# Seven block products in place of eight for the up products of five FFNs on one core

## The chip, the cores and the metric

One core of one Trainium2 chip runs the whole program. The metric is the device time in microseconds (us) of one execution. The engines are named as in the profile: PE multiplies matrices (PEld is its weight loads), ACT is ScalarE, DVE is VectorE, POOL is GpSimd, and SP issues the transfers.

## What is computed

Two transformer layers and one further block run on 512 tokens of width 1024 (a context of 256 tokens is used in the first layer). Six feed-forward networks (FFNs, here 0 to 5) carry most of the arithmetic:

```
D_MODEL = 1024
SEQ = 512
D_FF = 2816
def swiglu(h, wi, wo):
    a, u = jnp.split(h @ wi, 2, axis=-1)
    return (jax.nn.silu(a) * u) @ wo
```

`h @ wi` is the up product (1024 to 2 x 2816), `@ wo` the down product. Between the FFNs stand a mixer of attention and a recurrent part, a pooling mixer and a second mixer. Each layer is steered by modulation vectors, `silu(cond) @ w_mod`, 216 columns of 128 in all (the kernel calls their work ada).

## The kernel before

All activations lie transposed: 128 features on the partitions, tokens along a row. A product in float32 is made of three matmuls (`mm3`, L181 to L184): weight high part times activation high part, weight high part times activation low part, weight low part times activation high part. High parts are made by ACT (a copy into fp32r, L177 for weights, L187 for activations), low parts by DVE as the difference (L178, L188). So every weight tile takes one ACT and one DVE instruction.

An FFN (`ffn`, L331) works through 22 blocks f of 128 hidden columns in four parts of 5, 5, 6 and 6 blocks. In a part it first makes the up products of its blocks (`run`, `up`), then the down products of that part for eight slices d of the output (`downs`). For a block, `up` multiplies eight input chunks by two 128-column halves (gate and up) and three terms: 48 matmuls of 512 columns into two PSUM banks (tile `pau`). Then `gate` (L357, L358, L187, L188) applies silu, multiplies and splits the result into `g`. A block's weights arrive in two transfers of 512 KB (`load_raw`, tile `wraw`, four buffers with the tag `raw`), and `split_w` makes `whi` and `wlo` of 1024 columns from each. The ada work (`ada_step`: one 512 KB load into a buffer of the same tag, one dot product on DVE over 1024 columns, L124) is spread over the blocks, two for each. FFNs 1 to 5 have only the stream x of 512 tokens; FFN 0 also has the context.

A scheduler orders the instructions of each engine. Each engine then runs its queue strictly in that order, so an instruction that waits holds everything behind it. Transfers are issued by SP, in one queue.

## Time and profile before

| what | us |
| --- | --- |
| median of 3 runs | 3187.15 |
| lowest and highest run | 3186.84, 3192.39 |
| the profiled execution, its own time | 3192.12 |
| its span, first to last instruction | 3190.3 |
| PE busy in the span | 3074.2 |
| DVE, ACT, POOL busy | 1764.8, 1144.0, 272.8 |

How to read it: the profile lists each engine's busy time, groups of equal instructions with the mean time of one and the idle time before them, and a chain that is followed back from the last instruction. An engine's instructions in order of time show when each started and how long it took. A matmul's listed time contains its passage through the array, so PE's pace is read from the distance of starts. All rows are from the one profiled execution.

### The profile page before, as it was taken

What the parts mean: (1) busy time and instruction counts of PE and PEld (TensorE: products, weight loads), DVE (VectorE), ACT (ScalarE), POOL (GpSimd) and SP (SyncE); (2) the same over time, 40 slices, a digit from 0 to 9 for tenths busy, and PEclk for the clock granted to TensorE, in tenths of its full rate; (3) what the DMA queues carried; (4) which work ended last, traced back from release to release, by engine and by line L of the source; (5) the groups of instructions that cost most, each with busy time, mean ns of one, the idle gap of its engine ahead of it and who ended that gap; (6) DMA issues with size and microseconds to landing.
All of it is one profiled execution on the core that took longest, in us unless ns stands there. A gap on an engine that the chain in (4) does not pass through costs nothing.

```text
span 3190.3 us, 41925 instructions
## 1 busy us (share of the span) xinstructions
PE 3074.2 (96%) x16678; PEld 2585.4 (81%) x16678; DVE 1764.8 (55%) x2952; ACT 1144.0 (36%) x1904; POOL 272.8 (9%) x263
## 2 busy tenths in 40 slices
PE   6899999999899999999997999999999999999998
PEld 4788888888678888888886888888888898788887
DVE  8875535535765555655457545555533557843334
ACT  4532212433543222522234322253223556632222
POOL 4300000211100000100003000010000221110000
PEclk8999999999999999999998999999999999999999
DMA  5653525111113454445451345534433221112331
GB/s 218 240 185 105 172 90 162 56 57 54 47 41 107 157 175 162 128 156 165 145 192 47 123 155 171 174 109 147 159 99 109 78 67 54 59 58 92 107 99 62
DMA packets 118040, 381.59 MB, mean 120 GB/s; under 512 B 13490, under 2 KB 17458, under 8 KB 117844
## 3 DMA queue, kind: packets, MB, share of 16 engines
q1 hardware_dynamic: 117844, 378.91, 36.7%
q8 instruction: 131, 2.15, 0.3%
q14 instruction: 65, 0.53, 0.1%
HBM read 376.76 MB, written 2.10 MB: 119 GB/s over the span
## 4 chain that ended last, share of the span: by engine, by line
PE 86%; DVE 8%; ACT 3%; issue 2%; POOL 1%; DMA 1%; DVEq 0%; ACTq 0%; POOLq 0%; SPq 0%
PE pau L183 15%; PE pau L184 15%; PE pau L182 15%; PE py L182 8%; PE py L183 8%; PE py L184 8%; PE pj L668 1%; PE pj L669 1%; PE pj L670 1%; PE pj L183 1%; PE pj L182 1%; PE pc L182 1%; PE pc L183 1%; PE pc L184 1%; PE pj L184 1%
## 5 line engine op out<-in xcount | busy, mean ns | idle before, releaser
L182 PE MATMUL pau<-hx,whi 128*128 128x512 f32 (+1 forms) x2272 | 864.9, 382 | 22.3 <-ACT hx L187 10.7
L183 PE MATMUL pau<-hx,whi 128*128 128x512 f32 (+1 forms) x2272 | 868.3, 382 | 6.5 <-DVE hx L188 4.4
L184 PE MATMUL pau<-hx,wlo 128*128 128x512 f32 (+1 forms) x2272 | 867.1, 382 | 0.0
L177 ACT ACTIVATE whi<-wraw 128x1024 fp32r<-128x1024 f32 (+2 forms) x538 | 510.2, 954 | 930.7 <-PE py L183 446.7
L178 DVE TENSOR_TENSOR wlo<-wraw,whi 128x1024 fp32r<-128x1024 f32 (+2 forms) x538 | 591.0, 1103 | 320.4 <-ACT whi L177 311.2
L182 PEld LDWEIGHTS pau<-hx,whi 128*128 128x128 f32 x2272 | 432.7, 191 | 110.8 <-ACT hx L187 12.0
L183 PEld LDWEIGHTS pau<-hx,whi 128*128 128x128 f32 x2272 | 433.5, 191 | 96.0 <-DVE hx L188 6.7
L184 PEld LDWEIGHTS pau<-hx,wlo 128*128 128x128 f32 x2272 | 433.4, 191 | 87.7 <-DVE wlo L178 0.4
L182 PE MATMUL py<-g,whi 128*128 128x512 f32 (+1 forms) x1376 | 492.1, 358 | 9.2 <-DVE x L371 7.1
L183 PE MATMUL py<-g,whi 128*128 128x512 f32 (+1 forms) x1376 | 489.2, 356 | 1.1 <-DVE g L188 1.1
L184 PE MATMUL py<-g,wlo 128*128 128x512 f32 (+1 forms) x1376 | 488.6, 355 | 0.0
L124 DVE CUSTOM_DVE_ANT_0 junk<-adaw,cv_c,cst 128x1024 bf16<-128x1024 f32 x192 | 246.5, 1284 | 204.5 <-DMA adaw<-in_ada 203.3
L371 DVE SCALAR_TENSOR_TENSOR x<-py,gate,x 128x512 f32<-128x512 f32 (+1 forms) x216 | 149.0, 690 | 290.3 <-PE py L184 289.4
L182 PEld LDWEIGHTS py<-g,whi 128*128 128x128 f32 x1376 | 259.2, 188 | 53.1 <-ACT hc L281 5.7
L183 PEld LDWEIGHTS py<-g,whi 128*128 128x128 f32 x1376 | 259.4, 189 | 41.2 <-DVE g L188 1.4
L184 PEld LDWEIGHTS py<-g,wlo 128*128 128x128 f32 x1376 | 259.1, 188 | 40.5
L357 ACT ACTIVATE sl<-pau 128x512 f32<-128x512 f32 x132 | 78.9, 598 | 519.0 <-PE pau L184 518.8
L358 DVE TENSOR_TENSOR sl<-sl,pau 128x512 f32<-128x512 f32 x132 | 90.7, 687 | 298.5 <-PE pau L184 279.4
L216 POOL TENSOR_TENSOR acc<-acc,sq 128x512 f32<-128x512 f32 (+1 forms) x33 | 43.1, 1309 | 2309.5 <-ACT sq L214 2309.3
L187 ACT ACTIVATE g<-sl 128x512 fp32r<-128x512 f32 (+1 forms) x154 | 92.4, 601 | 112.6 <-DVE sl L358 110.6
L668 PE MATMUL pj<-whi,hx 128*128 128x256 f32 x448 | 129.3, 289 | 0.3 <-ACT vtok L675 0.3
L669 PE MATMUL pj<-whi,hx 128*128 128x256 f32 x448 | 126.5, 282 | 0.0
(417 smaller groups left out, 3630.6 us busy)
## 6 DMA issues: line engine op xcount, KB each, us to landing
wraw<-in_wi SPq DMA_DIRECT2D x274, 512.0 KB, 3.4
adaw<-in_ada SPq DMA_DIRECT2D x192, 512.0 KB, 3.8
wraw<-in_wo SPq DMA_DIRECT2D x96, 384.0 KB, 3.1
wraw<-in_wo SPq DMA_DIRECT2D x104, 320.0 KB, 3.0
wraw<-in_w_in SPq DMA_DIRECT2D x42, 512.0 KB, 3.4
adas<-in_ada SPq DMA_DIRECT2D x32, 512.0 KB, 6.2
wraw<-in_w_out SPq DMA_DIRECT2D x16, 512.0 KB, 3.4
wraw<-in_ada SPq DMA_DIRECT2D x8, 512.0 KB, 4.1
```

The costliest lines, as they stand in the source:

```text
L124: V.tensor_tensor_reduce(junk, raw, cvec(vec), 1.0, C(f"b{l}", c, 1), OP.mult, OP.add, mods[dst][:, c:c + 1])
L177: S.activation(hi, raw, AF.Copy)
L178: V.tensor_tensor(lo, raw, hi.bitcast(F32), OP.subtract)
L182: PE.matmul(o, wh, xh, start=start, stop=False)
L183: PE.matmul(o, wh, xl, start=False, stop=False)
L184: return PE.matmul(o, wl, xh, start=False, stop=stop)
L187: a = S.activation(hi, src, AF.Copy)
L357: S.activation(sl, o[0], AF.Silu)
L358: V.tensor_tensor(sl, sl, o[1], OP.mult)
L371: V.scalar_tensor_tensor(s.x[d][:, c0:c1], py[:, :c1 - c0], s.gate[:, d:d + 1], s.x[d][:, c0:c1], op0=OP.mult, op1=OP.add)
L668: PE.matmul(o, xh, hi[:, k % 4, :], start=k == 0, stop=False)
L669: PE.matmul(o, xl, hi[:, k % 4, :], start=False, stop=False)
```

## The change

In parts 1 to 3 of FFNs 1 to 5 a block's up product is treated as a 2 by 2 block matrix product: weights a11, a21 (gate and up columns of input chunks 0 to 3), a12, a22 (of chunks 4 to 7), and activations cut into chunks 0 to 3 and 4 to 7 by tokens 0 to 255 and 256 to 511. Seven products of 256 columns are made (`seven`), each of 4 chunks and 3 terms, so 84 matmuls of 256 columns stand where 48 of 512 stood. Their operands are sums:

- `combine_h`, once in an FFN, makes eight combined activation tiles (`todd`, `teven`) in part 0: for each of four k, four instructions on POOL, two on DVE, and two splits.
- `weight_sums`, once for a block, makes four sums of weight tiles (`ws`) on POOL, each 128x512.
- `form` splits the seven weight tiles of a block (three raw, four sums), 128x512 each, on ACT (L405) and DVE (L406). Form i of the next block is made behind product i of this one.
- Behind the products, ACT copies four partial results out of PSUM (L431 to L439), since one bank (`ba`) collects products 0, 2, 4 and 6 one after the other; DVE adds two and multiplies one (L437, L442, L446), POOL adds one and multiplies one (L440, L444).

One ada step goes with each of these blocks and one with each down slice of parts 0 to 2. The tile `g` has 6 buffers in place of 7. Some small pads and the buffer count of one vector change too.

```
     def gate(s, f, o):
...
+        def combine_h(k):
...
+            b1, b2, odd, even = (tmp([T], name="tc") for _ in range(4))
+            for b, c in ((b1, k), (b2, 4 + k)):
+                hh = hs["x"][c].bitcast(F32)
+                G.tensor_tensor(b, hh[:, 0], hh[:, 1], OP.add)
+            lo_, hi_ = slice(0, 256), slice(256, 512)
+            G.tensor_tensor(odd[:, lo_], b1[:, hi_], b1[:, lo_], OP.subtract)
+            V.tensor_tensor(even[:, lo_], b2[:, hi_], odd[:, lo_], OP.subtract)
+            G.tensor_tensor(odd[:, hi_], b2[:, hi_], b1[:, hi_], OP.subtract)
+            V.tensor_tensor(even[:, hi_], b2[:, lo_], even[:, lo_], OP.subtract)
+            for src, name in ((odd, "odd"), (even, "even")):
+                split(src, tt[name][k][:, 0], tt[name][k][:, 1])
+
+        def weight_sums(f):
+            w0, w1 = (load_raw(A[f"wi{n}"][f, p], [4, 2, 128]) for p in range(2))
+            a11, a21, a12, a22 = w0[:, :, 0], w0[:, :, 1], w1[:, :, 0], w1[:, :, 1]
+            s1, s2, s3, s4 = (tt["pool"].tile([128, 4, 128], F32, name="ws", tag="ws", bufs=4) for _ in range(4))
+            G.tensor_tensor(s1, a21, a22, OP.add)
+            G.tensor_tensor(s2, s1, a11, OP.subtract)
+            G.tensor_tensor(s3, a11, a21, OP.subtract)
+            G.tensor_tensor(s4, a12, s2, OP.subtract)
+            return [a11, s1, s2, a12, s3, s4, a22]
+
+        def form(src):
+            if not slot:
+                t = [wp.tile([128, 2, 4, 128], F32R, name=nm, tag=nm, bufs=4) for nm in ("whi", "wlo")]
+                slot.extend([(t[0][:, i], t[1][:, i]) for i in range(2)])
+            hi, lo = slot.pop(0)
+            S.activation(hi, src, AF.Copy)
+            V.tensor_tensor(lo, src, hi.bitcast(F32), OP.subtract)
+            return hi, lo
+
+        def seven(f, w, then):
...
+            def product(i, o, start):
+                hi, lo = w[i]
+                for k in range(4):
+                    mm3(o, hi[:, k], lo[:, k], mv[i](k, 0), mv[i](k, 1), start and k == 0, k == 3, not start)
+
+            for i, (o, start) in enumerate(((ba, True), (bc, True), (ba, False), (bd, True), (ba, False), (bc, False),
+                                            (ba, False))):
+                product(i, o, start)
+                with tc.high_priority():
+                    if i == 0:
+                        S.activation(q1[:, first], ba, AF.Copy)
+                    elif i == 1:
+                        S.activation(q1[:, second], bc, AF.Copy)
+                    elif i == 2:
+                        S.activation(q2[:, first], ba, AF.Copy)
+                    elif i == 3:
+                        V.tensor_tensor(a[:, first], bd, q1[:, first], OP.add)
+                    elif i == 4:
+                        S.activation(q2[:, second], ba, AF.Copy)
+                        G.tensor_tensor(q1[:, second], q1[:, second], q2[:, second], OP.add)
+                    elif i == 5:
+                        V.tensor_tensor(a[:, second], bc, q2[:, first], OP.add)
+                        S.activation(a, a, AF.Silu)
+                        G.tensor_tensor(a[:, second], a[:, second], q1[:, second], OP.mult)
+                    else:
+                        V.tensor_tensor(a[:, first], a[:, first], ba, OP.mult)
+                        ins = split(a, g[:, 0, :], g[:, 1, :])
+                then(i)
+            return ins
...
+                    if not cx:
+                        for k in {2: (0, 1), 3: (2,), 4: (3,)}[f]:
+                            combine_h(k)
                     ada_step(steps if X in ss and not (start and pi == 0) else 0, last_gate, pi == 0 and f == 2)
+
+            def run_seven(fs):
+                nonlocal last_gate
+                del slot[:]
+                src = weight_sums(fs[0])
+                w = [form(x) for x in src]
+                for f in fs:
+                    nxt_w = []
+                    src = weight_sums(f + 1) if f + 1 in fs else []
+                    last_gate = seven(f, w, lambda i: nxt_w.append(form(src[i])) if src else None)
+                    ada_step(1, last_gate)
+                    w = nxt_w
...
                     hi, lo = load_w(A[f"wo{n}_{pi}"][d], [nk, 128])
+                    if not cx and not last:
+                        ada_step(1)
...
-            run(todo)
+            if pi and not cx:
+                run_seven(fs)
+            else:
+                run(todo)
+            if last and not cx:
+                closed(f"tt{n}")
```

Three queues show the order around the second block of part 1 of FFN 1. In the rows `wraw` is a raw weight tile, `ws` a sum, `sq7` the partial results of a block, `pau` and `pd` its PSUM banks, `adaw` an ada column. First DVE, before, around the gate (L358, L188) of a block of that part:

```order
L178 TENSOR_TENSOR wlo_9190<-wraw_9187,whi_9189 128x1024
L358 TENSOR_TENSOR sl_9173<-sl_9173,pau_9124 128x512
L124 ISA junk_9333,mod_c1_76<-adaw_9331,cv_c_8764,cst_67 128x1024
L124 ISA mod_c1_76 128x1
L188 TENSOR_TENSOR g_9174<-sl_9173,g_9174 128x512
L178 TENSOR_TENSOR wlo_9196<-wraw_9193,whi_9195 128x1024
L124 ISA junk_9337,mod_c1_76<-adaw_9335,cv_c_8764,cst_67 128x1024
L124 ISA mod_c1_76 128x1
```

and DVE after, in the later half of the second block (the rows named 9392), up to the first two forms of the block after next:

```order
L437 TENSOR_TENSOR sq7_9392<-pd_9389,sq7_9390 128x256
L124 ISA junk_9653,mod_c1_76<-adaw_9651,cv_c_8807,cst_67 128x1024
L124 ISA mod_c1_76 128x1
L406 TENSOR_TENSOR wlo_9473<-ws_9381,whi_9472 128x512
L406 TENSOR_TENSOR wlo_9473<-ws_9382,whi_9472 128x512
L442 TENSOR_TENSOR sq7_9392<-pau_9388,sq7_9391 128x256
L446 TENSOR_TENSOR sq7_9392<-sq7_9392,pau_9387 128x256
L406 TENSOR_TENSOR wlo_9509<-wraw_9377,whi_9508 128x512
L406 TENSOR_TENSOR wlo_9509<-wraw_9516,whi_9508 128x512
L189 TENSOR_TENSOR g_9393<-sq7_9392,g_9393 128x512
L406 TENSOR_TENSOR wlo_9564<-ws_9520,whi_9563 128x512
L406 TENSOR_TENSOR wlo_9564<-ws_9521,whi_9563 128x512
```

A block had four pieces of its own and two dot products on DVE; it has eleven and one. POOL before, in FFN 1: the norm ahead of it (`mt`) is followed at once by the squares of its last down slices (`acc`), so POOL has nothing in parts 1 to 3 up to there:

```order
L275 TENSOR_TENSOR mt_8502<-x3_81,rs_y_8485 128x256
L275 TENSOR_TENSOR mt_8511<-x5_83,rs_y_8485 128x256
L275 TENSOR_TENSOR mt_8520<-x7_85,rs_y_8485 128x256
L216 TENSOR_TENSOR acc_10810<-acc_10810,sq_10847 128x512
L216 TENSOR_TENSOR acc_10810<-acc_10810,sq_10882 128x512
L216 TENSOR_TENSOR acc_10810<-acc_10810,sq_10917 128x512
```

POOL after, in the same second block (the L440 and L444 of 9392) and the start of the third:

```order
L394 TENSOR_TENSOR ws_9520<-wraw_9516,wraw_9518 128x512
L395 TENSOR_TENSOR ws_9521<-ws_9520,wraw_9516 128x512
L440 TENSOR_TENSOR sq7_9390<-sq7_9390,sq7_9391 128x256
L396 TENSOR_TENSOR ws_9522<-wraw_9516 128x512
L397 TENSOR_TENSOR ws_9523<-wraw_9518,ws_9521 128x512
L444 TENSOR_TENSOR sq7_9392<-sq7_9392,sq7_9390 128x256
L394 TENSOR_TENSOR ws_9659<-wraw_9655,wraw_9657 128x512
L395 TENSOR_TENSOR ws_9660<-ws_9659,wraw_9655 128x512
```

The block's gate product (L444) stands behind four weight sums for the block after next. ACT before, around two gates of that part:

```order
L177 ACTIVATE whi_9195<-wraw_9193 128x1024
L187 ACTIVATE g_9174<-sl_9173 128x512
L177 ACTIVATE whi_9265<-wraw_9263 128x1024
L357 ACTIVATE sl_9249<-pau_9199 128x512
L177 ACTIVATE whi_9271<-wraw_9269 128x1024
L187 ACTIVATE g_9250<-sl_9249 128x512
```

ACT after, at the end of the second block and the start of the third (9531, pau_9528):

```order
L439 ACTIVATE sq7_9391<-pau_9387 128x256
L405 ACTIVATE whi_9472<-ws_9382 128x512
L443 ACTIVATE sq7_9392<-sq7_9392 128x512
L405 ACTIVATE whi_9508<-wraw_9377 128x512
L405 ACTIVATE whi_9508<-wraw_9516 128x512
L188 ACTIVATE g_9393<-sq7_9392 128x512
L431 ACTIVATE sq7_9531<-pau_9528 128x256
L405 ACTIVATE whi_9563<-ws_9520 128x512
```

The copy of the third block's first partial result (L431) stands behind the split of the second block's gate (L188), which reads what L444 on POOL writes.

## Rows read from the trace of the kernel before

**Rows 1.** The page: PE's busy line, and the chain by engine.

```profile
PE 3074.2 (96%) x16678; PEld 2585.4 (81%) x16678; DVE 1764.8 (55%) x2952; ACT 1144.0 (36%) x1904; POOL 272.8 (9%) x263
...
PE 86%; DVE 8%; ACT 3%; issue 2%; POOL 1%; DMA 1%; DVEq 0%; ACTq 0%; POOLq 0%; SPq 0%
```

**Rows 2.** Stretches: downs, ups of FFN 1 (parts 0, 1, 2); FFN 5's part 1.

```profile
core 0: us, PE busy (x) PEld busy (x) DVE busy (x) ACT busy (x) POOL busy (x), PEclk, DMA share, GB/s
1019.70:1047.70 28.00, 28.00 (x122) 22.57 (x121) 16.37 (x21) 7.58 (x11) 0.00 (x0) 1.00 0.45 142
1047.70:1103.70 56.00, 56.00 (x242) 45.05 (x241) 26.74 (x36) 14.56 (x20) 0.00 (x0) 1.00 0.52 164
...
1131.70:1198.60 66.90, 66.90 (x290) 54.24 (x289) 33.27 (x44) 18.00 (x23) 0.00 (x0) 1.00 0.55 175
...
2891.90:2947.70 55.80, 55.80 (x242) 45.25 (x241) 16.93 (x19) 14.41 (x19) 0.00 (x0) 1.00 0.25 79
```

**Rows 3.** PE's groups in FFN 1's parts 1 to 3: busy, mean, idle before.

```profile
L182 PE MATMUL pau<-hx,whi 128*128 128x512 f32 x272 | 107.4, 395 | 0.0
```

**Rows 4.** PE in order of time (start, us): FFN 1's 256-column start, part 2's ups.

```profile
968.86 0.37 PE L182 MATMUL pau<-hx,whi 128*128 128x256 f32 x1
...
986.09 0.40 PE L182 MATMUL pau<-hx,whi 128*128 128x512 f32 x1
...
1131.67 0.39 PE L182 MATMUL pau<-hx,whi 128*128 128x512 f32 x1
...
1198.60 0.40 PE L182 MATMUL py<-g,whi 128*128 128x512 f32 x1
```

**Rows 5.** DVE's groups over the whole span: busy, mean ns.

```profile
L124 DVE CUSTOM_DVE_ANT_0 junk<-adaw,cv_c,cst 128x1024 bf16<-128x1024 f32 x192 | 246.5, 1284 | 204.5 <-DMA adaw<-in_ada 203.3
L371 DVE SCALAR_TENSOR_TENSOR x<-py,gate,x 128x512 f32<-128x512 f32 x168 | 126.1, 750 | 279.7 <-PE py L184 279.1
...
L188 DVE TENSOR_TENSOR g<-sl,g 128x512 fp32r<-128x512 f32 x132 | 91.1, 692 | 15.7 <-ACT g L187 15.7
...
L358 DVE TENSOR_TENSOR sl<-sl,pc 128x256 f32<-128x256 f32 x22 | 9.1, 415 | 0.0
```

**Rows 6.** ACT's groups over the whole span, as rows 5.

```profile
L187 ACT ACTIVATE g<-sl 128x512 fp32r<-128x512 f32 x132 | 83.2, 632 | 78.5 <-DVE sl L358 76.5
...
L357 ACT ACTIVATE sl<-pc 128x256 f32<-128x256 f32 x22 | 8.1, 367 | 0.0
```

**Rows 7.** POOL in order of time (start us, us), FFN 0's first blocks.

```profile
37.62 3.41 POOL L511 TENSOR_TENSOR adas<-adas,cv_c_ctx 128x1024 f32<-128x1024 f32 x1 [2.62 <-DVE mod_c L124]
41.66 2.33 POOL L275 TENSOR_TENSOR mt<-x,rs_y 128x512 f32<-128x512 f32 x1 [0.62 <-DVE gs L603]
...
47.95 1.29 POOL L275 TENSOR_TENSOR mt<-x,rs_y 128x512 f32<-128x512 f32 x1 [0.63 <-DVE mod_cc L516]
...
111.47 0.74 POOL L216 TENSOR_TENSOR acc<-acc,sq 128x256 f32<-128x256 f32 x1 [12.54 <-ACT sq L214]
...
131.83 2.41 POOL L511 TENSOR_TENSOR adas<-adas,cv_c_ctx 128x1024 f32<-128x1024 f32 x1 [10.17 <-DMA adas<-in_ada]
```

**Rows 8.** DVE in order of time, in the same stretch.

```profile
38.73 2.85 DVE L188 TENSOR_TENSOR hx<-mt,hx 128x512 fp32r<-128x512 f32 x1
...
41.58 1.27 DVE L124 CUSTOM_DVE_ANT_0 junk<-adas,cv_c,cst 128x1024 bf16<-128x1024 f32 x1
...
91.32 1.88 DVE L188 TENSOR_TENSOR g<-sl,g 128x512 fp32r<-128x512 f32 x3
...
111.38 0.68 DVE L358 TENSOR_TENSOR sl<-sl,pau 128x512 f32<-128x512 f32 x1
```

**Rows 9.** The page's DMA issues: KB of one, us to landing.

```profile
wraw<-in_wi SPq DMA_DIRECT2D x274, 512.0 KB, 3.4
```

**Rows 10.** Stretches as rows 2: in FFN 0, and between FFNs 2 and 3.

```profile
60.00:110.00 50.00, 45.19 (x168) 35.23 (x169) 43.22 (x61) 24.92 (x41) 15.18 (x5) 0.87 0.67 234
...
1690.00:1748.00 58.00, 36.81 (x204) 31.88 (x203) 45.70 (x100) 27.41 (x60) 24.73 (x28) 0.79 0.09 31
```

More of the change, by code (lines that the diff above doesn't have):

```diff
@@ L334, in ffn @@
         gp = opened(f"g{n}")
-        ada_pool[0] = gp
+        ada_pool[:] = gp, 1 if n else 2
+        if n != 2:
+            gp.tile([128, 16], F32, name="pad", tag="pad")
         psum = opened_psum(f"pf{n}")
@@ new lines, in ffn @@
+        tt, slot = {}, []
+        def combine_h(k):
+            if k == 0:
+                pool = tt["pool"] = opened(f"tt{n}")
+                pool.tile([128, 16], F32, name="pad", tag="pad")
+                tt["odd"], tt["even"] = [[pool.tile([128, 2, T], F32R, name=f"t{a}{i}") for i in range(4)]
+                                         for a in ("odd", "even")]
+            b1, b2, odd, even = (tmp([T], name="tc") for _ in range(4))
[9 more added lines that the diff above has]
+                split(src, tt[name][k][:, 0], tt[name][k][:, 1])
@@ new lines, in form @@
+        def form(src):
[7 more added lines that the diff above has]
+        def seven(f, w, then):
+            h = hs["x"]
+            first, second = slice(0, 256), slice(256, 512)
+            ba, bc = (psum.tile([128, T], F32, name="pau", tag="au", bufs=4)[:, first] for _ in range(2))
+            bd = psum.tile([128, T], F32, name="pd", tag="m")[:, first]
+            mv = [lambda k, p: h[k][:, p, first], lambda k, p: tt["odd"][k][:, p, first],
+                  lambda k, p: tt["even"][k][:, p, first], lambda k, p: h[4 + k][:, p, first],
+                  lambda k, p: tt["odd"][k][:, p, second], lambda k, p: h[4 + k][:, p, second],
+                  lambda k, p: tt["even"][k][:, p, second]]
+            q1, q2, a = (tmp([T], name="sq7") for _ in range(3))
+            g = new_g(X, f)
+            def product(i, o, start):
[26 more added lines that the diff above has]
+            return ins
@@ L489, in program @@
     xs = [act.tile([128, T], F32, name=f"x{d}") for d in range(KC)]
-    opened("top", side="right").tile([128, 8], F32, name="pad", tag="pad")
+    opened("top", side="right").tile([128, 24], F32, name="pad", tag="pad")
     hpool = opened("hp0", side="right")
     hcpool = opened("hc", side="right")
-    hcpool.tile([128, 8], F32, name="pad", tag="pad0")
     adp = opened("ad", side="right")
```

22 lines of the change are left out of this document (13 added, 9 removed).

## The prediction

> **What bounds the kernel now.** I read the page first: PE is busy 96% of the span and carries 86% of the chain of work [rows 1]. Then the stretches of one FFN: in FFN 1's up and down stages PE is busy for the whole of every stretch at a granted clock of 1.00, with POOL empty and DVE at about half (26.74 of 56.00 us in part 1) [rows 2]. The groups of PE there show 0.0 us of idle before their matmuls [rows 3]. So these stages last as long as their matmuls take, and everything else fits beside them. A matmul's pace comes from starts: from 1131.67 to 1198.60 six blocks, 288 matmuls of 512 columns, are begun, 66.93 us or 232 ns each; from 968.86 to 986.09 144 matmuls of 256 columns, 17.23 us or 119.7 ns each [rows 4]. A block of before is thus 11.15 us.
>
> **PE's part of the change.** 48 matmuls of 512 columns go, 84 of 256 come: 84 x 0.1197 = 10.05 us. That is 1.10 us a block, and with 17 blocks in each of five FFNs (85) 94 us, if PE remains the bound.
>
> A rule speaks against halving the columns, since the weight loads rise from 48 to 84. The rows show loads hidden at both widths: the starts at 256 columns are 119.7 ns apart, with a load for each [rows 4]. The Trainium skill (TensorE: Matmul & The Clock Gate, section "Part 3: Packing small matmuls — row/col tiling") says that a load overlaps a running matmul only where the row groups differ, and the same page prices a load of 128 columns at about 107 ns. By it, a full-array load would add itself to each matmul, and a block would go from 48 x (213 + 107) to 84 x (107 + 107) ns, an estimate from that page of 2.6 us more for each block. The trace contradicts it and decides, so it gets no chance below.
>
> **What POOL and DVE have to do.** POOL gets, for each block, four sums of 128x512 and two pieces of 128x256. Undisturbed these take 1.29 and 0.74 us [rows 7]: 6.6 us. DVE gets seven forms and one g split of 128x512, three pieces of 128x256 that read PSUM, and in FFNs 1 to 3 one ada dot. Back to back a 128x512 split takes 0.60 us ((1.88 - 0.69) / 2) [rows 5, 8], the dot 1.28, the PSUM pieces 0.42 each [rows 5]: 8 x 0.60 + 1.28 + 3 x 0.42 = 7.3 us. Each alone is under 10.05 us. The question is whether they run side by side, and the early part of the trace says no. A split of 128x512 takes 0.69 us, but the one that starts at 38.73 takes 2.85: a POOL instruction runs from 37.62 to 41.03, and the split ends 0.55 us behind it [rows 5, 7, 8]. It goes both ways: that POOL instruction takes 3.41 us, where one of the same shape takes 2.41 alone, as a dot on DVE was ahead; the next, 128x512, takes 2.33 in place of 1.29 and ends 1.14 us after the dot that began at 41.58 [rows 7, 8]. An instruction of DVE that reads PSUM is not held: 0.68 us at 111.38, while POOL works [rows 7, 8]. So a split or a dot (two operands from SBUF) and a POOL sum take turns, and whichever is second waits for the whole of the other.
>
> The Trainium skill draws the same line for placing work: Perfetto Trace Analysis says that GpSimd and VectorE share a read port of SBUF, so that moving work from one to the other might not help. By it POOL's sums cost DVE's time; without it they would be free beside the matmuls, which is rival A below. The trace bears the rule out.
>
> With turns taken, a block needs at least 4 x 1.14 + 2 x 0.60 (0.74 less the 0.15 that 1.29 loses) on POOL and 8 x 0.55 + 1.28 on DVE, 5.76 + 5.68 = 11.4 us with an ada dot and 10.2 without; with the undisturbed durations 6.6 + 6.1 = 12.7 and 11.4. PE's 10.05 us is below all of these, and 11.15 is what is to be beaten.
>
> **Why waits come on top.** The lag can't be carried far, because of the queues. In a block that prepares sums for the block after next, POOL's queue is four sums, one add (L440), and last the gate product (L444); ACT's split of the gate (L188) waits for it, and behind L188 on ACT stands L431, the copy of the next block's first product, for which PE's third product waits, since both use one bank. I walk one such block with ada, time zero at the start of its third product. The first sum needs a weight tile whose buffer is freed by a split at about 0.3; its transfer lands 3.4 us later [rows 9], so the sum starts at 3.8. From there POOL's 5.76 us, and in turn with them the dot and three or four forms of DVE (1.28 + 3 x 0.55 = 2.9): L444 ends at 12.5. Then L188 0.63, L431 0.37 [rows 6], in every second block one more form 0.63 between them, and some semaphores: the next third product starts at 13.6 to 14.3. Without ada the loads come a block earlier, the first sum starts at 1.25 behind a form, and 5.76 + 6 x 0.55 put L444's end at 10.3 and the next third product at about 11.5. The last two blocks of a part prepare no sums and take PE's 10.05.
>
> **The sum.** Of 17 blocks in an FFN 11 prepare sums (3, 4, 4) and 6 do not. In FFNs 1 to 3 (47 ada steps each, in place of 40) I take 13.4 us, between the demand of 11.4 and the walk's 14.3, nearer to the walk, as it follows the queues: 11 x (13.4 - 11.15) - 6 x 1.10 = +18 us an FFN, +54. In FFNs 4 and 5, where no ada is left, 11 x 0.35 - 6.6 = -2.7 each, -5. Part 0's combined tiles cost POOL 8 x 1.29 + 8 x 0.74 = 16 us and DVE about 8, beside three blocks and a down stage, 61 us: nothing on PE. The down stages of parts 0 to 2 take on eight dots (10.3 us) and the first block's forms and sums: DVE's 16.37 of 28.00 us [rows 2], less four weight splits of the next part (some 4.9), plus 10.3 + 4.8, is 26.6, and POOL's 5 to 9 us hold parts of it, less the residual adds (L371, 0.75 each, PSUM) that need not wait. That comes out between fitting and 3 us over; I take 1 for each of nine, +9. Total +58 on the profiled execution's 3192.1: 3250. The median of the runs shown lies 5 us lower, so **3245 us**. The forecast's own range, from 12.5 to 14.3 with ada, 10.6 to 12 without and 0 to 3 for a down stage: 3190 to 3305.
>
> **Rivals.**
> A. The turns vanish beside PE: DVE and POOL lag inside a part and catch up in its last two blocks. Then 94 us are gained: 3095. For it: no wait of PE now [rows 3]. Against: the demand of 11.4 to 12.7, and L431 behind L188, which leaves a lag less than one block. 0.10.
> B. Only the demand counts, not the waits: the sums start early and DVE's forms fall between POOL's chain of dependent instructions. Blocks that prepare take 11.4 with ada and PE's 10.05 without (10.2 is next to it): 3 x (11 x 0.25 - 6.6) - 2 x 17 x 1.10 = -49: 3140, faster. It decides at POOL's gate product L444: if it ends by 8.6 us after the third product's start in FFNs 4 and 5 (10.05 less the 1.4 of L188, L431 and semaphores), PE isn't held there. For it: no transfer gates those FFNs; against: the walk's 10.3. 0.15.
> C. The stalls, 2 to 3 us in each block, lower the granted clock. It was 0.87 in a stretch where PE was idle a tenth of the time and 0.79 where it was idle a third [rows 10]. At 0.9 in the 33 blocks with the longest stalls, 10.05 becomes 11.2: +37 us, 3285; at 0.8 over all preparing blocks 55 x 2.5 = +138. I take 3300. 0.14.
> D. The gain and the waits cancel to within 0.2%, the forecast with 12.3 in place of 13.4 and 11.0 in place of 11.5. 0.06.
>
> **Chances and range.** Forecast 0.55, A 0.10, B 0.15, C 0.14, D 0.06. A measurement of this kernel can tell about 0.2% from no change, 6 us. Faster: A and B and 0.02 of the forecast's low end, 0.27. Same: D and a little of the forecast, 0.07. Slower: 0.66. The range keeps B, leaves out A and about half of C: 3125 to 3310.
>
> **What would show it.** Right: in a preparing block PE's third product waits for ACT's L431, ACT's L188 for POOL's L444; the weight sums on POOL last clearly over 1.29 us on average and DVE's L406 over 0.69; a block of FFN 1 spans 12.5 to 14.3 us, the last two of a part about 10.1; FFNs 4 and 5 come out shorter than FFNs 1 to 3. Wrong: POOL's sums near 1.29 and DVE's forms near 0.69 (no turns), or long ones but no idle time on PE (A); L444 done by 8.6 us (B); PEclk under 1.00 in the up stages (C). A pace of PE other than 119.7 ns at 256 columns would upset the gain itself.

## The result, and the profile after

The changed kernel takes 3316.07 us (median of 4 runs, 3311.24 to 3320.97), the kernel before 3188.28 in the same comparison: 1.040 times as long, 95% interval 1.038 to 1.042. The forecast of 3245 had the direction right and less than half of the size: +58 us against +128, and 6 us above the range. The profiled execution has a span of 3314.7 us (before 3190.3).

The page's busy line and chain, which answer [rows 1]:

```profile
PE 3016.6 (91%) x19738; PEld 2699.6 (81%) x19738; DVE 2228.4 (67%) x3627; ACT 1434.5 (43%) x2708; POOL 1063.5 (32%) x853
...
PE 58%; DVE 16%; POOL 8%; ACT 7%; DMA 6%; issue 6%; SPq 0%; DVEq 0%; POOLq 0%; ACTq 0%
```

PE has 58 us less to do, the span is 124 us longer, and PE's share of the chain falls from 86% to 58%. The stretches that answer [rows 2]: the first down stage and the up stages of parts 1 and 2 of FFN 1, then FFN 5's part 1.

```profile
core 0: us, PE busy (x) PEld busy (x) DVE busy (x) ACT busy (x) POOL busy (x), PEclk, DMA share, GB/s
1015.20:1054.80 39.60, 32.30 (x121) 24.97 (x120) 31.19 (x44) 11.07 (x18) 10.87 (x8) 0.87 0.67 209
1054.80:1119.80 65.00, 52.86 (x422) 52.03 (x421) 49.87 (x71) 29.58 (x60) 32.35 (x25) 0.92 0.43 132
1148.20:1226.40 78.20, 64.37 (x506) 63.31 (x505) 59.34 (x83) 36.71 (x74) 40.99 (x30) 0.93 0.45 136
3011.80:3068.30 56.50, 50.30 (x422) 49.69 (x421) 37.86 (x51) 29.97 (x61) 26.78 (x22) 1.00 0.27 82
```

The stages of FFN 1 that are shown here had PE busy throughout; now they have holes, and in three of the four lines the mean granted clock is below 1.00. One of PE's waits over the whole span (total, times, longest) stands far above all others and names the place:

```profile
PE pau L183 <- ACT sq L431: 153.7, 58, 8.1
```

The stages' lengths, from PE's starts, in us. "Up" is parts 1 to 3; "first down" is the down stage of part 0 in FFNs 1 to 3. PE's own time is 17 blocks of 9.90 us an FFN. The rows after the first two are the experiments below; their medians were each taken beside runs of the kernel before (3187 to 3191).

| kernel | median | up, FFNs 1-3 | up, FFNs 4-5 | first down | ratio to before, interval |
| --- | --- | --- | --- | --- | --- |
| before | 3188 | 570.1 | 379.2 | 83.3 | |
| changed | 3316 | 657.1 | 393.3 | 117.8 | 1.040, 1.038-1.042 |
| no sums | 3120 | 507.9 | 337.2 | 115.3 | 0.978, 0.976-0.979 |
| gate on DVE | 3248 | 614.2 | 371.8 | 119.2 | 1.018, 1.016-1.020 |
| sums on DVE | 3170 | 551.8 | 349.0 | 114.9 | 0.993, 0.992-0.995 |
| combined tiles on DVE | 3298 | 665.7 | 394.1 | 96.9 | 1.033, 1.032-1.035 |
| all three on DVE | 3105 | 522.2 | 336.5 | 98.2 | 0.973, 0.972-0.975 |
| sums and combined tiles on DVE | 3153 | 550.5 | 349.5 | 96.9 | 0.988, 0.987-0.990 |
| same, no ada in first downs | 3163 | 554.5 | 356.0 | 88.0 | 0.991, 0.990-0.993 |
| no ada in the blocks | 3295 | 601.0 | 403.0 | 117.7 | 1.033, 1.031-1.034 |
| products exchanged | 3296 | 650.9 | 385.1 | 116.0 | 1.034, 1.032-1.036 |
| all on DVE, exchanged | 3126 | 531.4 | 353.7 | 97.6 | 0.981, 0.979-0.982 |
| four copies for the sums | 3146 | 541.6 | 344.7 | 117.0 | 0.987, 0.986-0.989 |
| eight copies | 3246 | 610.2 | 372.1 | 116.5 | 1.018, 1.017-1.020 |

The span's 124 us are: up stages of FFNs 1 to 3 +87.0, of FFNs 4 and 5 +14.0, first down stages of all five +33.4, later down stages -1.5, part 0's up stages and everything else -8.6.

**One block as it was walked.** FFN 5, no ada left. PE (the wait before it in brackets), POOL and ACT in order of time, start and duration in us:

```profile
3027.28 0.39 PE L183 MATMUL pau<-teven,whi 128*128 128x256 f32 x1 [2.60 <-ACT sq L431]
...
3038.74 0.39 PE L183 MATMUL pau<-teven,whi 128*128 128x256 f32 x1 [1.30 <-ACT sq L431]
```
```profile
3028.55 1.30 POOL L394 TENSOR_TENSOR ws<-wraw 128x512 f32<-128x512 f32 x1 [2.77 <-DVE wlo L406]
3030.54 1.64 POOL L395 TENSOR_TENSOR ws<-ws,wraw 128x512 f32<-128x512 f32 x1 [0.69 <-DVE wlo L406]
3032.69 0.97 POOL L440 TENSOR_TENSOR sq<-sq,sq 128x256 f32<-128x256 f32 x1 [0.51 <-ACT sq L439]
3033.62 1.74 POOL L396 TENSOR_TENSOR ws<-wraw 128x512 f32<-128x512 f32 x1
3035.33 1.29 POOL L397 TENSOR_TENSOR ws<-wraw,ws 128x512 f32<-128x512 f32 x1
3036.57 1.18 POOL L444 TENSOR_TENSOR sq<-sq,sq 128x256 f32<-128x256 f32 x1
```
```profile
3037.78 0.63 ACT L188 ACTIVATE g<-sq 128x512 fp32r<-128x512 f32 x1 [1.53 <-POOL sq L444]
3038.32 0.36 ACT L431 ACTIVATE sq<-pau 128x256 f32<-128x256 f32 x1
```

From one third product to the next: the first sum starts at 1.27 (the walk said 1.25), L444 ends at 10.47 (10.3), the next third product starts at 11.46 (11.5). The chain is the predicted one, link by link. One link counts for more than in the prediction, which had the first sum alone start behind a form: here two sums wait for DVE's forms (2.77 and 0.69 us), since a sum's tile is free only when the form of the block before has read it, and a form comes only behind its product. The agreement in total is partly luck: where the walk had 3.3 us of turns (6 x 0.55), POOL's six instructions take 8.12 us in place of 5.76, 2.4 more, and wait 1.2 us in between (0.69 for a form, 0.51 for ACT).

The block shown is of the short kind, and most are not. Of the 22 intervals of FFNs 4 and 5 in which sums are made five take 11.46 to 11.48 us. In every second interval (12 of the 22, 12.3 to 12.8 us) the first sum starts 2.0 to 2.8 us after the third product in place of 1.27, L444 ends at 10.8 to 11.3, and ACT makes one more form between L188 and L431. In the other five (12.75 to 13.02 us) the wait before was followed by 12 to 16 slow matmuls (see the clock below). The mean of all 22 is 12.4 us.

**The same place in FFN 1's part 1**, POOL between the third products at 1057.64 and 1075.24:

```profile
1058.86 1.68 POOL L396 TENSOR_TENSOR ws<-wraw 128x512 f32<-128x512 f32 x1 [2.43 <-DVE wlo L406]
1060.51 1.74 POOL L397 TENSOR_TENSOR ws<-wraw,ws 128x512 f32<-128x512 f32 x1
1065.02 1.67 POOL L394 TENSOR_TENSOR ws<-wraw 128x512 f32<-128x512 f32 x1 [2.77 <-DVE wlo L406]
1066.77 1.28 POOL L395 TENSOR_TENSOR ws<-ws,wraw 128x512 f32<-128x512 f32 x1
1068.01 2.25 POOL L396 TENSOR_TENSOR ws<-wraw 128x512 f32<-128x512 f32 x1
1070.21 1.17 POOL L440 TENSOR_TENSOR sq<-sq,sq 128x256 f32<-128x256 f32 x1
1071.35 1.70 POOL L397 TENSOR_TENSOR ws<-wraw,ws 128x512 f32<-128x512 f32 x1
1073.02 0.72 POOL L444 TENSOR_TENSOR sq<-sq,sq 128x256 f32<-128x256 f32 x1
```

Six sums stand here, not four: the last two of the second block are late from the down stage, and the third block's four follow. This first interval of the part lasts 17.60 us. In parts 1 and 2 of FFNs 1 to 3 the first interval always holds six sums and lasts 16.8 to 18.2 us; in part 3 it holds four and lasts 13.6 to 14.3. The next ones here take 13.75 and 13.38, and the 24 later intervals of FFNs 1 to 3 with sums 13.4 on average, near the walk's 13.6 to 14.3; but 0.9 of these 13.4 us is the slow clock, which the walk did not have.

**The clock.** PE's stretches (length, busy, count, granted clock, DMA share, GB/s): in FFN 1, before, in and after that wait, then a shorter wait in FFN 5 and what follows it.

```profile
1056.50:1067.50 11.00, 11.00 (x96) 1.00 0.46 144
1067.50:1075.20 7.70, 0.19 (x2) 0.67 0.46 136
1075.20:1080.60 5.40, 5.36 (x26) 0.52 0.35 100
1080.60:1084.70 4.10, 4.10 (x38) 1.00 0.29 92
3108.10:3110.80 2.70, 0.29 (x3) 1.00 0.64 194
3110.80:3114.70 3.90, 3.87 (x20) 0.56 0.45 137
```

Behind the wait PE works on at the lower of its two levels (0.52 is about 1.2 GHz): starts are 0.213 us apart in place of 0.118, as in these PE rows from FFN 5:

```profile
3111.29 0.41 PE L183 MATMUL pau<-teven,whi 128*128 128x256 f32 x1
3111.50 0.42 PE L184 MATMUL pau<-teven,whi 128*128 128x256 f32 x1
```

Counted over the starts of the 15 changed up stages, 356 matmuls are that slow, 356 x 0.095 = 34 us; before there was none in up stages. So the 208.8 us by which these stages exceed PE's own 841.5 are 34 of slow starts and, as what is left, 175 of waits.

**Part 0's down stage in FFN 1.** ACT, then SP's issues, then DVE, then PE:

```profile
1023.69 0.74 ACT L178 ACTIVATE whi<-wraw 128x640 fp32r<-128x640 f32 x1 [6.92 <-DMA wraw<-in_wo]
1024.33 0.58 ACT L362 ACTIVATE sl<-pau 128x512 f32<-128x512 f32 x1
```
```profile
1016.97 0.33 SPq L141 DMA_DIRECT2D adaw<-in_ada  x1
1019.39 0.33 SPq L154 DMA_DIRECT2D wraw<-in_wo  x1
```
```profile
1014.63 2.31 DVE L124 CUSTOM_DVE_ANT_0 junk<-adaw,cv_c,cst 128x1024 bf16<-128x1024 f32 x1
...
1017.99 1.34 DVE L179 TENSOR_TENSOR wlo<-wraw,whi 128x640 fp32r<-128x640 f32 x1
```
```profile
1026.60 1.22 PE L183 MATMUL py<-g,whi 128*128 128x512 f32 x2 [3.28 <-ACT g L188]
```

A dot takes 2.31 us in place of 1.28, as POOL makes the combined tiles beside it. It frees its raw buffer at 1016.9; only then does SP issue the next ada load, and behind it in SP's queue, at 1019.39, a load of down weights. That load needs a buffer of its own, which the split L179 frees at 1019.33; the split stands behind the dot in DVE's queue and takes 1.34 us, where the next one takes 0.81. ACT waits 6.92 us for this load, and behind ACT's wait stands the silu (L362) of the last block, whose `g` every down product of this part needs: PE waits 3.28 us for it.

### The profile page after: what moved, and what is told of

It is laid out like the page before. It is cut to its first block, busy times and chain, and to the rows that moved or that the text cites. A ratio compares the mean times of both kernels' runs of the same rounds, so it can differ in the third digit from the quotient of the medians.

```text
span 3314.7 us, 50616 instructions
## 1 busy us (share of the span) xinstructions
PE 3016.6 (91%) x19738; PEld 2699.6 (81%) x19738; DVE 2228.4 (67%) x3627; ACT 1434.5 (43%) x2708; POOL 1063.5 (32%) x853
## 4 chain that ended last, share of the span: by engine, by line
PE 58%; DVE 16%; POOL 8%; ACT 7%; DMA 6%; issue 6%; SPq 0%; DVEq 0%; POOLq 0%; ACTq 0%
PE pau L183 7%; PE pau L184 7%; PE pau L185 7%; PE py L184 6%; PE py L183 6%; PE py L185 6%; DVE wlo L406 4%; DMA adaw<-in_ada 3%; POOL ws L397 2%; DVE junk L124 2%; ACT whi L405 2%; POOL ws L396 2%; DVE wlo L179 2%; POOL sq L444 1%; DMA wraw<-in_wi 1%
## 5 line engine op out<-in xcount | busy, mean ns | idle before, releaser
L183 PE MATMUL pau<-hx,whi 128*128 128x256 f32 (+1 forms) x1592 | 518.3, 328 | 24.9 <-ACT hx L188 13.2
L184 PE MATMUL pau<-hx,whi 128*128 128x256 f32 (+1 forms) x1592 | 517.3, 325 | 4.9 <-DVE hx L189 3.0
L178 ACT ACTIVATE whi<-wraw 128x1024 fp32r<-128x1024 f32 (+3 forms) x368 | 329.6, 904 | 440.2 <-PE py L184 226.0
L185 PE MATMUL pau<-hx,wlo 128*128 128x256 f32 (+1 forms) x1592 | 516.7, 325 | 0.0
L179 DVE TENSOR_TENSOR wlo<-wraw,whi 128x1024 fp32r<-128x1024 f32 (+3 forms) x368 | 397.6, 1087 | 175.7 <-ACT whi L178 174.2
L406 DVE TENSOR_TENSOR wlo<-ws,whi 128x512 fp32r<-128x512 f32 x340 | 294.2, 874 | 99.6 <-ACT whi L405 90.8
L183 PE MATMUL pau<-teven,whi 128*128 128x256 f32 x680 | 208.5, 307 | 153.8 <-ACT sq L431 153.7
L183 PEld LDWEIGHTS pau<-hx,whi 128*128 128x128 f32 x1592 | 304.0, 191 | 51.4 <-ACT hx L188 14.5
L184 PEld LDWEIGHTS pau<-hx,whi 128*128 128x128 f32 x1592 | 303.5, 191 | 32.6 <-DVE hx L189 5.6
L405 ACT ACTIVATE whi<-ws 128x512 fp32r<-128x512 f32 x340 | 212.1, 626 | 230.2 <-PE pau L184 153.0
L183 PEld LDWEIGHTS pau<-teven,whi 128*128 128x128 f32 x680 | 137.4, 202 | 167.0 <-ACT sq L431 166.9
L406 DVE TENSOR_TENSOR wlo<-wraw,whi 128x512 fp32r<-128x512 f32 x255 | 255.5, 1014 | 9.4 <-ACT whi L405 0.4
```

The source lines that it names most:

```text
L178: S.activation(hi, raw, AF.Copy)
L179: V.tensor_tensor(lo, raw, hi.bitcast(F32), OP.subtract)
L183: PE.matmul(o, wh, xh, start=start, stop=False, skip_group_check=more)
L184: PE.matmul(o, wh, xl, start=False, stop=False, skip_group_check=more)
L185: return PE.matmul(o, wl, xh, start=False, stop=stop, skip_group_check=more)
L405: S.activation(hi, src, AF.Copy)
```

## The experiments

**1. What the sums cost as a whole.**

```
-            G.tensor_tensor(s1, a21, a22, OP.add)
...
-            G.tensor_tensor(s4, a12, s2, OP.subtract)
-            return [a11, s1, s2, a12, s3, s4, a22]
+            return [a11, a21, a21, a12, a11, a12, a22]
```

> This kernel leaves out POOL's four weight sums of each block: the products that should take a sum take a raw quarter of the weights, so the output is not the reference's. All forms, all products, the gate's pieces, the ada dots and the transfers stay. Theory (turns of DVE and POOL, and the gate product behind the sums in POOL's queue): with the sums gone both causes go, and every block falls to PE's 10.05 us or up to 10.5. The up stages of FFN 1 go from 65.0, 78.1 and 75.4 us to 50 to 53, 60 to 63 and 60 to 63, those of FFN 5 from 56.5, 69.6 and 69.5 to the same; over the five FFNs about 180 us, 3316 to about 3135, at most 3165. Rival (the loads of weight tiles gate the blocks, as POOL's wait for them would have it): a block with an ada transfer stays near 13 us, the kernel above 3270. Rival (the products' own chain through one bank, PE to ACT's copy to PE): blocks stay at 11 us or more in all FFNs, about 3200.

This kernel leaves out the sums. 3120 us, up stages 845 us for 85 blocks, 9.94 each: PE's pace. All 58 waits but 1.4 us in five are gone, though all transfers and ada steps are there. The loads do not gate the blocks, nor does the one bank by itself; the sums on POOL cost 196 us.

**2. The gate's two pieces to DVE.**

```
-  G.tensor_tensor(q1[:, second], q1[:, second], q2[:, second], OP.add)
+  V.tensor_tensor(q1[:, second], q1[:, second], q2[:, second], OP.add)
-  G.tensor_tensor(a[:, second], a[:, second], q1[:, second], OP.mult)
+  V.tensor_tensor(a[:, second], a[:, second], q1[:, second], OP.mult)
```

> The two pieces of the gate that POOL had (the add L440 and the product L444, 128x256 each) go to DVE; POOL keeps the four sums. Theory (the gate product queued behind POOL's sums, ACT's split behind it, the copy L431 behind that): the turns stay, but the chain to PE's third product is cut; blocks fall to the demand of the turns, 11.4 us with an ada dot and about 10.2 without. FFN 1's up stages together go from 218 us to 186 to 200, FFN 5's from 196 to 172 to 180; the kernel from 3316 to about 3170, between 3160 and 3240. Rival (only the demand of the turns counts, whoever holds the gate product): DVE gets 0.8 us more, POOL 1.2 us less, within 20 us of 3316. Rival (loads gate): no change, 3300 to 3320.

3248 us: 68 gained, less than half of the 146 expected and a little outside the range. FFN 5's intervals between third products are 11.0 and 11.9 us, not 10.2. POOL's queue is one part of the chain only: the gate's pieces now stand in DVE's queue behind forms that take turns with the same sums. In one block of FFN 5 a form takes 1.78 us beside a sum, the add L442 stands behind it, and ACT's silu waits for that:

```profile
3069.26 0.63 ACT L443 ACTIVATE sq<-sq 128x512 f32<-128x512 f32 x1 [2.53 <-DVE sq L442]
```

**3. The sums to DVE.**

```
-            G.tensor_tensor(s1, a21, a22, OP.add)
+            V.tensor_tensor(s1, a21, a22, OP.add)
...
-            G.tensor_tensor(s4, a12, s2, OP.subtract)
+            V.tensor_tensor(s4, a12, s2, OP.subtract)
```

> The four weight sums of a block go from POOL to DVE, 128x512 each; POOL keeps the gate's two pieces. Theory (turns and queue): nothing is left on POOL that holds DVE for long; DVE's own demand is 12 operations of 128x512 at 0.60 us, the dot of 1.28 and three PSUM pieces of 0.42, 9.7 us with ada and 8.5 without, both under PE's 10.05; blocks fall to 10.05 to 10.8. FFN 1's up stages together 218 to 172 to 185, FFN 5's 196 to 171 to 175; the kernel 3316 to about 3145, between 3130 and 3190. Rival (DVE becomes the bound, its sums late before the forms that wait for them, with 9.7 us of work in 10.05): FFNs 4 and 5 fall, FFNs 1 to 3 stay at 12 us or more, 3230 to 3270. Rival (loads gate): 3290 to 3320.

3170 us, 146 gained, inside the theory's range, and faster than before by 0.7% (0.5 to 0.8). FFNs 4 and 5 come to 10.3 us a block, FFNs 1 to 3 to 10.8. Neither rival's number fits.

**4. The combined tiles to DVE.**

```
-                G.tensor_tensor(b, hh[:, 0], hh[:, 1], OP.add)
+                V.tensor_tensor(b, hh[:, 0], hh[:, 1], OP.add)
...
-            G.tensor_tensor(odd[:, lo_], b1[:, hi_], b1[:, lo_], OP.subtract)
+            V.tensor_tensor(odd[:, lo_], b1[:, hi_], b1[:, lo_], OP.subtract)
...
-            G.tensor_tensor(odd[:, hi_], b2[:, hi_], b1[:, hi_], OP.subtract)
+            V.tensor_tensor(odd[:, hi_], b2[:, hi_], b1[:, hi_], OP.subtract)
```

> Only part 0 is touched: the adds and subtractions that POOL does for the combined tiles of the tokens (L381 to L385, two of 128x512 and two of 128x256 for each of four) go to DVE. Theory (the time that part 0 and its down stage lost, about 34 us in all, mostly 8 to 12 us between the last up product and the first dense down product of FFNs 1 to 3, comes from the ada dots and splits that wait for POOL's turns, which frees the raw buffers late and delays the loads of the down weights): DVE gets 4 x (2 x 0.60 + 2 x 0.35) = 7.6 us more of work but no waits; the gaps in FFNs 1 to 3 shrink to 2 to 5 us, the kernel from 3316 to 3285 to 3305. Rival (the loads themselves are too many in that stretch, whoever computes): within 5 us of 3316. Rival (DVE is full there, and the added work lengthens the gap): 3320 to 3345.

3298 us, 18 gained; the first down stages fall from 38 to 40 us to 32, while the up stages behind them grow by 8.6 us in FFNs 1 to 3. Some 7 of these are waits of 1.8, 2.2 and 3.0 us ahead of the first block's third product in part 1, where the changed kernel has none; their cause stays open. DVE's dots of that stretch of FFN 1 (1000 to 1050), first in the changed kernel, then here, busy us and mean ns:

```profile
L124 DVE CUSTOM_DVE_ANT_0 junk<-adaw,cv_c,cst 128x1024 bf16<-128x1024 f32 x13 | 19.2, 1474 | 1.0 <-DMA adaw<-in_ada 1.0
```
```profile
L124 DVE CUSTOM_DVE_ANT_0 junk<-adaw,cv_c,cst 128x1024 bf16<-128x1024 f32 x14 | 17.9, 1276 | 0.7 <-DMA adaw<-in_ada 0.6
```

DVE has more to do, and its dots are at their 1.28 us again.

**5. All three on DVE** (the edits of 2, 3 and 4 together).

> All that POOL does in the changed stages goes to DVE: the four weight sums, the gate's two pieces (L440, L444) and the combined tiles of part 0. In the kernel with the sums alone on DVE (3170 us) third products still wait 0.3 us in FFNs 4 and 5 and 1 to 2 us in FFNs 1 to 3, for ACT's copy L431 behind L188 behind POOL's L444, which takes 1.0 us there. Theory (the gate's detour over POOL is what is left of the chain): each piece takes 0.42 us on DVE, the third product starts 0.5 to 1 us earlier, and part 0 gives 18 us as it did alone; 3170 - 18 - 20 to 40: 3115 to 3135. Rival (DVE is the bound now): 12 operations of 128x512 at 0.60, the dot of 1.28 and five pieces of 0.42 are 10.6 us in FFNs 1 to 3, over PE's 9.9; those blocks stay at 10.8 or grow to 11.5, and the kernel is above the one that leaves the gate on POOL, 3150 to 3180.

3105 us, 2.7% faster than before (2.5 to 2.8): the fastest of all kernels here. FFNs 4 and 5 run at PE's 9.90 in nearly every block. DVE is busy for 58.35 of 60.70 us in FFN 1's part 2 and PE still for 60.22 (second line; first FFN 1's part 1, third FFN 5's), all at clock 1.00:

```profile
1047.20:1098.10 50.90, 50.17 (x422) 49.26 (x421) 48.95 (x90) 29.94 (x61) 0.00 (x0) 1.00 0.50 159
1129.70:1190.40 60.70, 60.22 (x506) 59.56 (x505) 58.35 (x109) 36.36 (x74) 0.00 (x0) 1.00 0.51 164
2831.30:2880.80 49.50, 49.50 (x421) 49.46 (x421) 39.50 (x73) 30.26 (x61) 0.00 (x0) 1.00 0.29 94
```

DVE's forms between 1050 and 2320, first in the changed kernel, then here:

```profile
L406 DVE TENSOR_TENSOR wlo<-ws,whi 128x512 fp32r<-128x512 f32 x204 | 175.9, 873 | 54.5 <-ACT whi L405 50.8
L406 DVE TENSOR_TENSOR wlo<-wraw,whi 128x512 fp32r<-128x512 f32 x152 | 161.6, 1075 | 5.6 <-ACT whi L405 0.4
```
```profile
L406 DVE TENSOR_TENSOR wlo<-ws,whi 128x512 fp32r<-128x512 f32 x246 | 164.6, 681 | 10.4 <-ACT whi L405 9.5
...
L394 DVE TENSOR_TENSOR ws<-wraw 128x512 f32<-128x512 f32 x61 | 42.0, 688 | 20.3 <-DMA wraw<-in_wi 18.9 <-DVE wlo L406 0.6
```

A sum takes 0.69 us on DVE; on POOL it took 1.36 to 1.76 and made the forms longer as well.

**6. Sums and combined tiles on DVE, the gate on POOL** (the edits of 3 and 4).

> The weight sums and part 0's combined tiles go to DVE, the gate's two pieces stay on POOL. Theory (the two losses are separate: turns and queue in the up stages, late raw buffers in part 0): the gains add up, 3170 - 18 = 3152, between 3140 and 3160, with the first down stage of FFNs 1 to 3 at 31 to 33 us in place of 37 to 39.5. Rival (in part 0 DVE is full with the sums of the next part beside the combined tiles): the first down stages stay at 36 us or more, 3165 to 3180.

3153 us: the two gains add up (3170 - 18). Against experiment 5, the gate's detour over POOL alone costs 48 us.

**7. As 6, no ada step in part 0's down stage.**

```
-                    if not cx and not last:
+                    if not cx and not last and pi:
                         ada_step(1)
```

> As the kernel before it in this call, and part 0's down stage issues no ada step (8 fewer in each of FFNs 1 to 3; they are made up later, by FFN 4's steps or ahead of the next modulation). Theory (what is left of part 0's loss, about 4 us in each of FFNs 1 to 3, is the wait of the down weights for raw buffers behind ada transfers and dots): the first down stages go to 28 to 29.5 us, 12 us in all; the moved steps cost up to as much elsewhere; 3140 to 3155. Rival (the rest is the combined tiles' own work on DVE and ACT ahead of the splits of the down weights): the first down stages stay at 31 to 33 us, and the kernel is the same or slower.

The first down stages fall from 32.3 to 29.3 us, as the theory had it, but the kernel takes 3163 us, over the range: the steps not made there are made in FFN 4, whose first down stage grows from 27.2 to 35.9 us and whose up stages by 6.6.

**8. No ada step in the changed blocks.**

```
                     last_gate = seven(f, w, lambda i: nxt_w.append(form(src[i])) if src else None)
-                    ada_step(1, last_gate)
...
-                    if not cx and not last:
-                        ada_step(1)
+                    if not cx:
+                        ada_step(2 if last else 1)
```

> The changed kernel, but with no ada step in the seven-product blocks; 16 of the 17 steps of an FFN go to the last down stage (two for each d), which follows the up stages. POOL keeps sums, gate and combined tiles. Theory (a preparing block is as long as the turns and the queue make it, and an ada dot and its transfer are a part of that, 1.3 us of a turn and a raw buffer): FFN 1's up stages go from 218 us to FFN 5's 196 to 204, in its second blocks from 20 us to about 14; the last down stage of FFNs 1 to 3 grows by 0 to 10 us each; the kernel 3316 to 3255 to 3295. Rival (the transfers alone make FFNs 1 to 3 slow and the turns cost nothing): FFN 1's up stages fall to 175 or less. Rival (ada has no part in it): 214 to 220.

3295 us. The up stages of FFNs 1 to 3 fall by 56, to 200 us an FFN, near FFN 4's and 5's 198 and 196 of the changed kernel; the 31 us that they still cost above the kernel before remain, with POOL's work as it was. The steps go to the last down stage of each FFN, and 35 of the 56 come back elsewhere, partly in FFN 4, which now still has ada steps (206.5 us in place of 197.7).

**9. The third and fourth products exchanged**, so that bank `ba` is taken again 1.43 us later; the forms follow the new order.

```
-  ((ba, True), (bc, True), (ba, False), (bd, True), (ba, False), ...
+  ((0, ba, True), (1, bc, True), (3, bd, True), (2, ba, False), (4, ba, False), ...
```

> The changed kernel with its third and fourth products exchanged, so that the bank of the first product is taken again 1.43 us (12 matmuls of 119 ns) later; the forms follow the new order, everything else stays on its engine. In the trace of the changed kernel PE waits 153.7 us in 58 waits for ACT's copy L431 of that bank. Theory (this reuse is the last link of the chain, but the time is set by the sums and the gate product ahead of it): the waits get up to 1.4 us shorter, at most 58 x 1.4 = 81 us, and a part comes back because the sums are paced by the forms and those by PE's products; 3316 to 3240 to 3290. Rival (the reuse of the bank is the cause by itself): the short waits of 1.6 us go and the long ones shrink fully, 3235 or less. Rival (only the work of the turns counts): within 12 us of 3316.

> Sums, gate pieces and combined tiles on DVE, and the third and fourth products exchanged. Without the exchange that kernel took 3105 us; its up stages in FFNs 4 and 5 are PE's own 9.9 us a block, those of FFNs 1 to 3 lose 17 us together, 0.4 to 1.4 us at a third product at a time. Theory (those are single waits for L431 that 1.4 us cover): 3088 to 3100. Rival (DVE's own work bounds FFNs 1 to 3): the waits move to another product, 3101 to 3110.

Neither came out. On the changed kernel 20 us were gained (3296, between the theory's range and the rival's bound); with all on DVE the exchange lost 21 (3126). The edit is no clean test: it brings the third and fifth products, both into `ba`, together. With all on DVE the scheduler put 8 of the sixth product's 12 matmuls between them, and still a product starts 0.05 us behind the copy it waits for, at two places of each block:

```profile
2872.51 0.37 ACT L435 ACTIVATE sq<-pau 128x256 f32<-128x256 f32 x1
...
2874.65 0.39 ACT L439 ACTIVATE sq<-pau 128x256 f32<-128x256 f32 x1 [1.25 <-PE pau L185]
```

PE's starts behind these copies are at 2872.94 and 2875.09. FFNs 4 and 5 lose 0.5 us a block, which they did not lose before the exchange. What the reuse of the bank costs by itself was not measured; experiment 1 shows that it costs nothing where the sums are gone.

**10. POOL's time, or POOL's second operand.** The four sums become four copies, then each copy is made twice.

```
-            G.tensor_tensor(s1, a21, a22, OP.add)
+            G.tensor_copy(s1, a21)
...
-            G.tensor_tensor(s4, a12, s2, OP.subtract)
+            G.tensor_copy(s4, a12)
```

> The changed kernel with POOL's four sums replaced by four copies of one operand each, 128x512, into the same tiles: this leaves out the sums, so the output is not the reference's. POOL's queue, the ws buffers, the forms and the gate stay. It asks what makes DVE's forms long (873 and 1075 ns on average in FFNs 1 to 3, against 681 with POOL idle): a second operand that POOL reads, or any work of POOL. If turns are taken for any POOL operation that reads SBUF: forms stay at 0.85 to 1.1 us, and the kernel between 3250 and 3316 by how long a copy is. If only operations of two operands take turns with DVE's: forms at 0.69, copies at their undisturbed time, the up stages of FFN 1 at 172 to 185 us and the kernel at 3130 to 3190, though the queue (gate product behind four POOL operations) is as before; that would make the turns, not the queue, the cause of most of it. If the queue alone costs the time: above 3270 with short forms.

> As the kernel with four copies in place of the sums, but each copy is made twice into the same tile: eight copies of 128x512 on POOL for each block (this leaves out the sums, so the output is not the reference's). Four sums take 6.2 us of POOL in a block of the changed kernel (1.36 + 1.52 + 1.76 + 1.54), four copies took 3.4 (0.77 + 0.86 + 0.98 + 0.79): with eight, 6.2 to 6.8, POOL's queue in front of the gate product is as long as with the sums. Theory (turns: DVE's forms are held by two-operand sums, far less by copies, 757 ns in place of 873): forms stay under 0.85 us on average, and the kernel comes out nearer to the one with four copies, 3150 to 3230. Rival (the time that POOL takes, whatever it does, through the gate product at the end of its queue): 3270 to 3330 with forms as short as with four copies. Between 3230 and 3270 both have a share.

Both kernels leave out the sums. 3146 and 3246 us. With four copies the time lies in the range of the second case (two operands only), the forms do not. POOL's four sums took 1.36 + 1.52 + 1.76 + 1.54 = 6.2 us a block, four copies 3.4, eight copies 6.5. Two of POOL's groups in the changed kernel; then DVE's forms with no sums (experiment 1), with four copies and with eight; then a copy and the form that runs beside it:

```profile
L396 POOL TENSOR_TENSOR ws<-wraw 128x512 f32<-128x512 f32 x85 | 149.7, 1761 | 58.5 <-DVE wlo L406 58.5
...
L394 POOL TENSOR_TENSOR ws<-wraw 128x512 f32<-128x512 f32 x85 | 115.5, 1359 | 460.8 <-DMA wraw<-in_wi 364.5 <-DVE wlo L406 96.3
```
```profile
L401 DVE TENSOR_TENSOR wlo<-wraw,whi 128x512 fp32r<-128x512 f32 x428 | 294.5, 718 | 50.3 <-ACT whi L400 37.7
```
```profile
L406 DVE TENSOR_TENSOR wlo<-ws,whi 128x512 fp32r<-128x512 f32 x237 | 176.3, 757 | 39.1 <-ACT whi L405 35.9
```
```profile
L410 DVE TENSOR_TENSOR wlo<-ws,whi 128x512 fp32r<-128x512 f32 x219 | 180.7, 837 | 45.2 <-ACT whi L409 41.1
```
```profile
2048.05 0.61 POOL L394 COPY ws<-wraw 128x512 f32<-128x512 f32 x1 [2.54 <-DVE wlo L406]
```
```profile
2048.09 1.12 DVE L406 TENSOR_TENSOR wlo<-ws,whi 128x512 fp32r<-128x512 f32 x1
```

With eight copies POOL's queue is as long as with the sums and the kernel is 70 us faster; doubling the copies costs 100. So of the 170 us between four copies and the sums, 100 go with POOL's time, 70 with what the sums do beyond it (the copies also read fewer raw tiles, which these runs do not separate). DVE's forms between 1050 and 2320 were 873 and 1075 ns with sums, 757 and 763 with four copies, 837 and 872 with eight. The gate's two-operand pieces are on POOL in all these runs; with them and no sums the forms take 718 ns, against 681 with POOL idle, so the copies' own share is what lies above 718. They do hold forms: the copy shown ends at 2048.66, and the form that starts beside it ends 0.55 us later. So turns are not a matter of two operands on POOL alone. The expectation for eight copies (forms under 0.85, up to 3230) is missed by a little on both counts; both causes have a share.

## Why the prediction was right in direction and wrong in size

- **PE's pace: right.** A block's own time is 9.90 us where 10.05 was taken, so 107.8 us of PE's time went, 94 predicted. The loads hide, as the 256-column rows said.
- **The turns: right.** DVE's forms and dots and POOL's sums all lengthen beside each other. Rival A (no turns felt) and rival B (only the demand) are excluded by the trace of the changed kernel: intervals with sums in FFNs 4 and 5 take 11.46 to 13.02 us, and L444 ends no earlier than 10.47, not by 8.6.
- **The sizes.** Against the forecast's +58 us the span's +124 is 66 more: 33 in the up stages of FFNs 1 to 3, 19 in those of FFNs 4 and 5, 30 in the first down stages, less 16 elsewhere.
- **The chain L444, L188, L431, third product: right**, and one block of FFN 5 follows the walk to 0.2 us. But the walked block was taken for all. The mis-sized terms are the 11.5 without ada and the start of a part with it. Without ada the intervals with sums take 12.4 on average: POOL starts later and ACT has one more form ahead of L431 in every second block, which the walk had counted with ada only (-5 us forecast for FFNs 4 and 5, +14.0 measured). With ada the 13.4 is the mean of 24 of the 33 intervals, though 0.9 of it is the slow clock that the forecast left out; the nine first ones take 16.2 on average (+25 us), and the blocks at the end of a part 11.1 in place of 10.05 (+9): +54 forecast, +87.0 measured. The sum had no state at the start of a part: the second block's sums, late from the down stage, lie in the same interval as the third's. That these two late sums make the long interval is read from the trace. Experiment 8 fits, for there at most one of them still starts in the interval, which takes 13.4 to 14.5 us in parts 1 and 2; but it moves the dots as well, so it does not single the sums out.
- **The clock: treated as a rival, was a consequence.** Rival C gave the stalls' effect on the clock a chance of its own, and the forecast's sum stood at full clock. C's sign came (0.92 and 0.93 in FFN 1's up stages) together with those of the forecast. The slow starts come behind PE's stalls: 34 us of the up stages, and 10 us of the down stages (50 matmuls at 0.43 us apart in place of 0.23), where before it was 2.4. Two mechanisms of which one causes the other cannot share out the chances; they have to be added. With the 34 alone, counted from starts and not separated by a run, the forecast is 3279.
- **Part 0: the step that failed outright.** "Nothing on PE" was argued from sums of busy time (POOL 16 us and DVE 8 in 61). It cost 34.5 us in FFNs 1 to 3 and nothing in 4 and 5. Experiment 4 shows that 21 of it are the combined tiles on POOL, experiment 7 that a further 9 are the ada steps of that down stage; the remaining 4 or 5 stay open. The path was through queues that the sum did not look at: a dot's turn, its raw buffer, SP's queue, ACT's queue.
- **Later down stages:** +1 us each forecast, about none measured. They carried their dots. That their cost appears as late sums in the next part is likely from the trace, and not shown by a run.
- **Rival D** does not add up as written: with 12.3 and 11.0 its sum is +11 us, not within 0.2%.

That the change pays with its sums on DVE was not seen: the work that made it lose is the sums on POOL, and with the same seven products DVE makes them in half the time.

The Trainium skill (Perfetto Trace Analysis, "Optimizing Scalar/DVE Operations") says of the shared port that moving operations between GpSimd and VectorE might not help. Here it helped, since a sum takes 0.69 us on DVE and 1.36 to 1.76 on POOL, and whoever makes it, the other waits. The Trainium skill (GPSIMD Engine Reference, section 4.1, "Engine selection") puts an operation with two inputs at about twice VectorE's time on GpSimd, and with one input near line rate; the trace agrees for two inputs, with 1.29 us for an operation of the sums' shape undisturbed [rows 7] against 0.69. For one input no run has the same copy on both engines; on POOL it took 0.61 us where least disturbed.

## What to carry to other kernels

Where two engines take turns, count an operation at its time on both, and put it on the engine that does it in less time, even if that engine is the busier one. When stalls are forecast, price the slower clock behind each of them as part of the same case, and walk the start of a stage apart from its middle, through every queue (the transfers' too) that a lengthened instruction holds up. A sum of busy times says that work fits only if nothing behind it in its queue is waited for.
